# A decoder layer on one core: the first weight tile in two column parts, and the gate multiplications without their order edge from the third block on

## The chip, the core and the metric

One core of one Trainium2 chip. The metric is the time of one execution in device microseconds, the median of several. An execution is one launch of the whole layer, with all weights read from HBM.

## What is computed

One decoder layer for 272 tokens (16 meta tokens and 256 others) of 2048 channels in float32. Cut to what matters here:

```python
h = layer_norm(concat(meta, x))                  # first stage: "h_hl" in the kernel
proj = h @ w_in                                  # 2048 x 8192, 64 weight tiles
a, zh, zb, zc, gates = split(proj)
ya = (pool_mixer(a) @ pool_w * pool_scale) @ pool_proj
yb = (zb * causal_conv(zc * zh)) @ conv_proj
h = layer_norm(alpha * h + (gates[0] * ya + gates[1] * yb) @ w_out)
# PEER: 128 experts per token are picked out of 16384, 16 for each of 8 heads
act = gelu(x . expert_u[idx]);  coef = gate * act
y = sum(coef * expert_v[idx])
out = layer_norm(alpha * h + y)[16:]
```

## The kernel before

**Number format.** Each float32 operand of a large product is split into a high and a low fp32r part (`whi`, `wlo` for weights, `c_hi`, `c_lo` for coefficients, `h_hl`, `x_hl` for activations), and a product is the sum of three: high by high, high by low, low by high. `mm3` (L102 to L104) issues three matmuls for a weight tile and a column range; `mm2` (L108, L109) issues two, the first of them over high and low activations side by side. ACT rounds a raw weight tile to `whi` (L95), DVE or, for some, POOL subtracts to get `wlo` (L74). `load` brings raw tiles of 1 MB into three buffers, issued by SP (L84); `whi` and `wlo` have three buffers of half a tile each.

**The first stage.** DVE normalises the rows. For each of two token tiles (144 tokens with the meta tokens, then 128) and each pair of 128-channel slices `k`, PE transposes into PSUM (L218, L219), ACT applies the norm's scale and shift into `ht` (L222), and DVE writes the high and low part of `h_hl` (L225, L74). Then `in_tile` multiplies the 64 tiles of `w_in`, each over 16 slices `k`. The first of them, with `cols0` = 14, covers columns 14 to 272 of the tokens: 258 columns by `mm3`, 48 matmuls. These want `h_hl` of both token tiles.

**The expert stage.** PEER goes over all 16384 experts as 128 rows of 128. For each row `e` there is an up and a down. The up (`up`) is 32 matmuls of `mm2` over 224 tokens; the 32 tokens left ("lone") are done by gathering rows (`urow`) and working on DVE. `both` (L112, L113) adds the two halves of an up into `gl`, and ACT applies gelu (L625). The down (`product`, L660) is three products of `c_hi`, `c_lo` with a tile of `expert_v`: 12 matmuls of 512 columns per row and half `dh` of the output channels. They accumulate in four banks `acc00` to `acc11`, or `mm` for the second half once the ups are over, and `add` (L669) adds the banks to `res`.

44 ups come ahead. Then the rows go in blocks of four (`NB`): block 0 begins near 957 us. A block is two ups, four downs of the first half, two ups, four downs of the second; ups end near 1830 us, then there are downs alone. `fetch` loads a block's gates `G` as seven DMAs of 64 KB on SP (L745) into one of two buffers. `coef(e)` (from L644) multiplies `gl` by its gate (L648, DVE), then ACT rounds to `c_hi` (L77) and DVE subtracts to `c_lo` (L74); coefficients have five buffers.

**What sets the order.** A scheduler orders each engine's instructions by estimated times and priorities, and each engine then runs its list strictly as it stands. `tc.issue_after(x)` is an edge: what is written in it may not stand ahead of instruction `x` on its engine. In `coef` the edge goes to `last_on["dve"]`, the last weight part or `both` that was recorded for DVE. `fetch(n)` needs a buffer of `Gp` free, so its DMAs wait until the last multiplication of block n - 2 has read it.

Of the kernel before, what the change touches and what calls it, by code (L numbers as in the profile page):

```python
# [18 lines left out]
P = 128  # L19
D = 2048  # L20
KD = D // P
T = 256
NT = T // P
META = 16
TT = T + META
WINDOWS = (2, 4, 8, 16)
# [9 lines left out]
NB = 4  # L36
# [17 lines left out]
def block(ctx, tc, x, meta, w_in, small, pool_w, projs, w_out, wq, keys, eu, eur, ev,  # L54
          ln1_g, ln1_b, ln2_g, ln2_b, lin_g, lin_b, out):
    nc = tc.nc

    def pool(stack, name, bufs, side="left"):
        return stack.enter_context(tc.tile_pool(name=name, bufs=bufs, side=side, reuse_waits="tile"))
# [7 lines left out]
    def ps_mm():  # L67
        return mm.tile([P, 512], F32, name="mm")

    def ps_acc(t, c):  # L70
        return accp.tile([P, 512], F32, name=f"acc{t}{c}")

    def lo_part(lo, full, hi, eng=None):
        return (eng or nc.vector).tensor_tensor(lo, full, hi.bitcast(F32), op=OP.subtract)  # L74

    def split(hi, lo, full):
        nc.scalar.copy(hi, full)  # L77
        lo_part(lo, full, hi)
# [3 lines left out]
    def load(src, shape=None):  # L82
        t = raws.tile([P, 2, 1024], F32, name="raw")
        last_load[0] = nc.sync.dma_start(t if shape is None else shape(t), src).ins  # L84
        return t

    last_lo = [None]
    last_on = {}

    def halves(parts, raw, lo_eng=None, lo_eng1=None, ahead=AHEAD):  # L90
        for s in range(2):
            hi = parts.tile([P, 1024], F32R, name="whi")
            lo = parts.tile([P, 1024], F32R, name="wlo")
            with tc.high_priority(offset=ahead):
                last_on["act"] = nc.scalar.copy(hi, raw[:, s]).ins  # L95
                eng = lo_eng1 if s and lo_eng1 else lo_eng
                last_lo[0] = lo_part(lo, raw[:, s], hi, eng)
                last_on["pool" if eng is nc.gpsimd else "dve"] = last_lo[0].ins
            yield hi, lo

    def mm3(ps, whi, wlo, xhi, xlo, first, last):
        nc.tensor.matmul(ps, whi, xhi, start=first, stop=False)  # L102
        nc.tensor.matmul(ps, whi, xlo, start=False, stop=False)  # L103
        nc.tensor.matmul(ps, wlo, xhi, start=False, stop=last)  # L104

    def mm2(ps, whi, wlo, xhl, first, last):
        n = xhl.shape[-1]
        nc.tensor.matmul(ps[:, :2 * n].rearrange("p (s t) -> p s t", s=2), whi, xhl, start=first, stop=False)  # L108
        nc.tensor.matmul(ps[:, :n], wlo, xhl[:, 0], start=False, stop=last)  # L109
# [60 lines left out]
    with ExitStack() as pa:  # L170
        a1 = pool(pa, "a1", 1, "right")
        parts = pool(pa, "parts", 3)
# [18 lines left out]
                       allow_small_or_imprecise_dtypes=True)  # L191
        nc.gpsimd.memset(neghalf, -0.5)

        h_hl = hp.tile([P, KD, 2, TT], F32R, name="h_hl")
        nc.scalar.activation(neghalf, neghalf, AF.Identity)
        srcs = ((mt[:META], META), (res[:, 0], P), (res[:, 1], P))
# [12 lines left out]
        for t in range(NT):  # L209
            t0, n = (META + P, P) if t else (0, META + P)  # L210
            for k0 in range(0, KD, 2):
                ps = ps_acc(k0 // 2 % 2, k0 // 4 % 2).rearrange("p (k t) -> p k t", k=2)
                ht = a2.tile([P, 2, META + P], F32, name="ht", bufs=4)
                for i in range(2):
                    k = k0 + i
                    ks = slice(k * P, (k + 1) * P)
                    if t == 0:
                        nc.tensor.transpose(ps[:, i, 0:META], mt[:META, ks], ident[:META, :META])  # L218
                    nc.tensor.transpose(ps[:, i, n - P:n], res[:, t, ks], ident)  # L219
                for i in range(2):  # L220
                    k = k0 + i
                    nc.scalar.activation(ht[:, i, :n], ps[:, i, :n], AF.Identity,  # L222
                                         bias=b_in[:, k:k + 1], scale=g_in[:, k:k + 1])
                h_hi = h_hl[:, k0:k0 + 2, 0, t0:t0 + n]
                nc.vector.tensor_copy(h_hi, ht[:, :, :n])  # L225
                lo_part(h_hl[:, k0:k0 + 2, 1, t0:t0 + n], ht[:, :, :n], h_hi)

        lg = lnp.tile([P, D], F32, name="lng")
        lb = lnp.tile([P, D], F32, name="lnb")

        wi = [0]

        later = []

        def in_tile(cols0):
            held = [f for n, f in later if n == 0]
            later[:] = [(n - 1, f) for n, f in later if n]
            ps = ps_mm()
            n = TT - cols0
            raw = load(w_in[wi[0]], lambda t: t.rearrange("p a b -> p (a b)"))  # L240
            wi[0] += 1
            for s, (hi, lo) in enumerate(halves(parts, raw)):
                for kk in range(8):
                    k = s * 8 + kk
                    cs = slice(kk * P, (kk + 1) * P)
                    if n == T:
                        mm2(ps, hi[:, cs], lo[:, cs], h_hl[:, k, :, cols0:], k == 0, k == KD - 1)
                    else:
                        mm3(ps[:, :n], hi[:, cs], lo[:, cs], h_hl[:, k, 0, cols0:], h_hl[:, k, 1, cols0:],
                            k == 0, k == KD - 1)  # L250
            for f in held:
                f()
            return ps if n == T else ps[:, :n]
# [6 lines left out]
        def group_product(g0, w):  # L260
            hi, lo = w
            for g in (g0, g0 + 1):
                for dt in range(2):
                    ps = ps_mm()
                    for ck in range(2):
                        o = (g % 2) * 512 + ck * 256 + dt * P
                        mm3(ps[:, :T], hi[:, o:o + P], lo[:, o:o + P], pooled[g][:, ck, 0], pooled[g][:, ck, 1],
                            ck == 0, ck == 1)
                    n = g * 2 + dt
                    y = a2.tile([P, T], F32, name="y")  # L270
                    nc.vector.tensor_scalar(y, ps[:, :T], scale_c[:, n:n + 1], None, op0=OP.mult)
                    split(ya[:, n, 0], ya[:, n, 1], y)

        for g, w in enumerate(WINDOWS):
            back = max(w, 2)
            a = a2.tile([P, 2, TT], F32, name="a")
            for j in range(2):
                nc.scalar.copy(a[:, j, META - back:], in_tile(META - back))
            prev, width = a, 1
            while width < w:  # L280
                cur = a2.tile([P, 2, TT], F32, name="win", bufs=2)
                lo_t = META - back + 2 * width - 1
                nc.vector.tensor_tensor(cur[:, :, lo_t:], prev[:, :, lo_t:],
                                        prev[:, :, lo_t - width:TT - width], op=OP.add)
                prev, width = cur, 2 * width
            po = a2.tile([P, 2, T], F32, name="po", bufs=1)
            nc.vector.scalar_tensor_tensor(po, prev[:, :, META:], 1.0 / w, a[:, :, META:],
                                           op0=OP.mult, op1=OP.subtract)
            p_hl = a2.tile([P, 2, 2, T], F32R, name="p_hl", bufs=2)
            split(p_hl[:, :, 0], p_hl[:, :, 1], po)  # L290
            pooled[g] = p_hl
            if g == 0:
                praw = load(pool_w, lambda t: t.rearrange("p a b -> p (a b)"))
            if g == 1:
                pw = halves(parts, praw)
            if g % 2 == 1:
                later.append((g // 2, lambda g=g: group_product(g - 1, next(pw))))
# [38 lines left out]
        for m in range(KD):  # L336
# [10 lines left out]
            for (hi, lo), y in zip(halves(parts, praw), (ya, yb)):  # L347
                ps = ps_mm()
                for k in range(NCH):
                    cs = slice(k * P, (k + 1) * P)  # L350
# [13 lines left out]
    with ExitStack() as pw:  # L364
        parts = pool(pw, "parts", 8 + 3)
# [190 lines left out]
    with ExitStack() as pb:  # L556
# [5 lines left out]
        parts = pool(pb, "parts", 3)  # L562
# [81 lines left out]
        def coef(e):  # L644
            gl = gels.pop(e)
            glv = gl.rearrange("p (g t) -> p g t", t=TG)
            with tc.issue_after(last_on["dve"]):
                nc.vector.tensor_tensor(glv, glv, Gs[e // NB][:, :, e % NB], op=OP.mult)  # L648
            c_hi = coefp.tile([P, TD], F32R, name="c_hi")
            c_lo = coefp.tile([P, TD], F32R, name="c_lo")  # L650
            split(c_hi, c_lo, gl)
            coefs[e] = (c_hi, c_lo)
# [248 lines left out]
```

## Time and profile before

| | |
|---|---|
| median of 3 runs | 2117.13 us (2116.28 to 2117.24) |
| profiled execution | 2117.67 us, span 2115.9 us |
| mean granted TensorE clock | 0.988 |
| PE busy | 2054.7 us, 97% |
| DVE busy | 1525.5 us, 72% |
| ACT busy | 1001.8 us, 47% |
| POOL busy | 600.8 us, 28% |
| chain that ended last | PE 90%, DVE 7%, issue, DMA, POOL and ACT 1% each |

The span is the time from the first to the last recorded instruction; the execution's own time has 1.8 us around it. Busy shares are means over stages that differ: the first 24 us and the last 16 us have hardly any matmul, near 700 us top-k work stands between, and in the expert stage PE is almost always busy.

### The profile page before, as it was taken

What the parts mean: (1) busy time and instruction counts of PE and PEld (TensorE: products, weight loads), DVE (VectorE), ACT (ScalarE), POOL (GpSimd) and SP (SyncE); (2) the same over time, 40 slices, a digit from 0 to 9 for tenths busy, and PEclk for the clock granted to TensorE, in tenths of its full rate; (3) what the DMA queues carried; (4) which work ended last, traced back from release to release, by engine and by line L of the source; (5) the groups of instructions that cost most, each with busy time, mean ns of one, the idle gap of its engine ahead of it and who ended that gap; (6) DMA issues with size and microseconds to landing.
All of it is one profiled execution on the core that took longest, in us unless ns stands there. A gap on an engine that the chain in (4) does not pass through costs nothing.

```text
span 2115.9 us, 29922 instructions
## 1 busy us (share of the span) xinstructions
PE 2054.7 (97%) x11558; PEld 1770.5 (84%) x11558; DVE 1525.5 (72%) x2340; ACT 1001.8 (47%) x1424; POOL 600.8 (28%) x294
## 2 busy tenths in 40 slices
PE   7999999999999699999999999999999999999997
PEld 6999888888888689998888888888888888877765
DVE  7766666666779878836767776776677677788878
ACT  5444544444443356554444444444444445444442
POOL 0000000000065588883332333232334232300001
PEclk9999999999999799999999999999999999999998
DMA  5555555566553357787878777878787877877654
GB/s 202 219 180 182 195 181 191 187 224 233 191 183 125 107 202 273 264 284 274 292 266 291 272 269 268 291 269 289 262 283 268 293 260 275 278 271 270 224 169 158
DMA packets 114334, 498.09 MB, mean 235 GB/s; under 512 B 11200, under 2 KB 38336, under 8 KB 73344
## 3 DMA queue, kind: packets, MB, share of 16 engines
q1 hardware_dynamic: 103584, 413.61, 56.8%
q0 software_dynamic: 10608, 82.58, 10.0%
q8 instruction: 90, 1.47, 0.3%
q14 instruction: 52, 0.43, 0.1%
HBM read 478.32 MB, written 16.78 MB: 234 GB/s over the span
## 4 chain that ended last, share of the span: by engine, by line
PE 90%; DVE 7%; issue 1%; DMA 1%; POOL 1%; ACT 1%; SPq 0%; POOLq 0%; ACTq 0%
PE mm L108 28%; PE acc L660 27%; PE mm L109 14%; PE mm L660 5%; PE mm L103 2%; PE mm L102 2%; PE mm L104 2%; PE acc L116 2%; PE acc L117 2%; PE acc L118 2%; PE mm L595 1%; POOL wlo L74 1%; DMA raw<-in_eu 0%; DVE res L669 0%; PE acc L219 0%
## 5 line engine op out<-in xcount | busy, mean ns | idle before, releaser
L95 ACT CAST whi<-raw 128x1024 fp32r<-128x1024 f32 x738 | 772.2, 1048 | 801.5 <-PE mm L108 256.4
L74 DVE TENSOR_TENSOR wlo<-raw,whi 128x1024 fp32r<-128x1024 f32 x546 | 684.7, 1257 | 471.8 <-ACT whi L95 468.3
L108 PE MATMUL mm<-x_hl,whi 128*128 128x448 f32 x2048 | 656.1, 379 | 18.6 <-DVE gl L113 16.8
L74 POOL TENSOR_TENSOR wlo<-raw,whi 128x1024 fp32r<-128x1024 f32 x192 | 490.9, 2563 | 587.1 <-ACT whi L95 282.9
L109 PE MATMUL mm<-x_hl,wlo 128*128 128x224 f32 x2048 | 544.4, 266 | 6.3 <-POOL wlo L74 6.1
L108 PEld LDWEIGHTS mm<-x_hl,whi 128*128 128x128 f32 x2048 | 387.7, 189 | 50.4 <-issue 17.2
L109 PEld LDWEIGHTS mm<-x_hl,wlo 128*128 128x128 f32 x2048 | 394.9, 193 | 10.3 <-POOL wlo L74 8.0
L660 PE MATMUL acc<-whi,c_lo 128*128 128x512 f32 (+1 forms) x832 | 260.7, 395 | 5.0 <-DVE c_lo L74 5.0
L660 PE MATMUL acc<-whi,c_hi 128*128 128x512 f32 (+1 forms) x832 | 260.8, 395 | 4.3 <-ACT c_hi L77 4.3
L660 PE MATMUL acc<-wlo,c_hi 128*128 128x512 f32 (+1 forms) x832 | 260.7, 395 | 0.0
L108 PE MATMUL mm<-h_hl,whi 128*128 128x512 f32 x640 | 225.0, 395 | 0.0
L136 POOL TENSOR_TENSOR rstd<-rstd,neghalf 128x1 f32<-128x1 f32 (+1 forms) x7 | 5.8, 821 | 713.8 <-DVE rstd L135 697.5
L660 PEld LDWEIGHTS acc<-whi,c_lo 128*128 128x128 f32 (+1 forms) x832 | 146.4, 176 | 52.7 <-DVE c_lo L74 6.4
L660 PEld LDWEIGHTS acc<-wlo,c_hi 128*128 128x128 f32 (+1 forms) x832 | 146.2, 176 | 46.1 <-issue 0.2
L660 PEld LDWEIGHTS acc<-whi,c_hi 128*128 128x128 f32 (+1 forms) x832 | 143.0, 176 | 47.5 <-ACT c_hi L77 4.8
L109 PE MATMUL mm<-h_hl,wlo 128*128 128x256 f32 x640 | 180.5, 282 | 0.0
L669 DVE SCALAR_TENSOR_TENSOR res<-res,acc 128x512 f32<-128x512 f32 x208 | 131.6, 679 | 22.6 <-PE acc L660 20.7
L108 PEld LDWEIGHTS mm<-h_hl,whi 128*128 128x128 f32 x640 | 120.4, 188 | 26.9
L625 ACT ACTIVATE gl<-gl 128x224 f32<-128x224 f32 x128 | 49.7, 389 | 168.8 <-DVE gl L113 168.8
L109 PEld LDWEIGHTS mm<-h_hl,wlo 128*128 128x128 f32 x640 | 121.3, 189 | 0.0
L103 PE MATMUL mm<-h_hl,whi 128*128 128x258 f32 (+3 forms) x384 | 110.4, 288 | 0.0
L102 PE MATMUL mm<-h_hl,whi 128*128 128x258 f32 (+3 forms) x384 | 109.3, 285 | 0.0
(189 smaller groups left out, 2586.4 us busy)
## 6 DMA issues: line engine op xcount, KB each, us to landing
raw<-in_eu SPq DMA_DIRECT2D x128, 1024.0 KB, 6.0
raw<-in_ev SPq DMA_DIRECT2D x128, 1024.0 KB, 5.6
raw<-in_w_in SPq DMA_DIRECT2D x64, 1024.0 KB, 4.9
raw<-in_projs SPq DMA_DIRECT2D x16, 1024.0 KB, 4.9
raw<-in_w_out SPq DMA_DIRECT2D x16, 1024.0 KB, 5.0
raw<-in_wq SPq DMA_DIRECT2D x16, 1024.0 KB, 4.8
spill<-wide POOLq DMA_DIRECT2D x7, 2048.0 KB, 7.9
G<-spill SPq DMA_DIRECT2D x212, 64.0 KB, 5.1
```

Source lines behind the costliest of these rows:

```text
L74: return (eng or nc.vector).tensor_tensor(lo, full, hi.bitcast(F32), op=OP.subtract)
L95: last_on["act"] = nc.scalar.copy(hi, raw[:, s]).ins
L102: nc.tensor.matmul(ps, whi, xhi, start=first, stop=False)
L103: nc.tensor.matmul(ps, whi, xlo, start=False, stop=False)
L104: nc.tensor.matmul(ps, wlo, xhi, start=False, stop=last)
L108: nc.tensor.matmul(ps[:, :2 * n].rearrange("p (s t) -> p s t", s=2), whi, xhl, start=first, stop=False)
L109: nc.tensor.matmul(ps[:, :n], wlo, xhl[:, 0], start=False, stop=last)
L116: nc.tensor.matmul(ps, xhi, whi, start=first, stop=False)
L117: nc.tensor.matmul(ps, xhi, wlo, start=False, stop=False)
L625: nc.scalar.activation(gl, gl, AF.Gelu)
L660: nc.tensor.matmul(ps[c][:n_t], c_[:, ts], v_[:, c * 512:(c + 1) * 512], start=e == first and n == 0, stop=e == last and n == 2)
L669: nc.vector.scalar_tensor_tensor(r, r, 1.0 if (t, dh, c) in added else ALPHA, ps[c][:n_t], op0=OP.mult, op1=OP.add)
```

## The change

Two edits. First, a generator `first_tile` multiplies the first tile of `w_in` in two column parts: columns 14 to 144 (130) are written behind the first token tile's transposes, columns 144 to 272 (128) behind the second's. The 48 matmuls of 258 columns become 96. The first `in_tile` call is left out and its bank taken from the generator (`begun`). Second, in `coef` the order edge of the gate multiplication stands only for the first two blocks (`e < 2 * NB`, eight rows); for the other 120 rows the scheduler may place it anywhere behind its inputs.

```diff
+        def first_tile():
+            cols0 = META - max(WINDOWS[0], 2)
+            ps = ps_mm()
+            raw = load(w_in[0], lambda t: t.rearrange("p a b -> p (a b)"))
+            wi[0] = 1
+            parts_ = list(halves(parts, raw))
+            for c0, c1 in ((cols0, META + P), (META + P, TT)):
+                for s, (hi, lo) in enumerate(parts_):
+                    for kk in range(8):
+                        k = s * 8 + kk
+                        cs = slice(kk * P, (kk + 1) * P)
+                        mm3(ps[:, c0 - cols0:c1 - cols0], hi[:, cs], lo[:, cs], h_hl[:, k, 0, c0:c1],
+                            h_hl[:, k, 1, c0:c1], k == 0, k == KD - 1)
+                yield ps[:, :TT - cols0]
...
+            if t == 0:
+                early.append(first_tile())
+            begun = next(early[0])
...
-                nc.scalar.copy(a[:, j, META - back:], in_tile(META - back))
+                nc.scalar.copy(a[:, j, META - back:], in_tile(META - back) if g or j else begun)
...
-            with tc.issue_after(last_on["dve"]):
+            with tc.issue_after(last_on["dve"]) if e < 2 * NB else ExitStack():
                 nc.vector.tensor_tensor(glv, glv, Gs[e // NB][:, :, e % NB], op=OP.mult)
```

PE has 48 matmuls more; all other engines have as many instructions as before. POOL's order is the same. Lines of the changed kernel are 18 or 19 higher (L648 is L667, L745 is L764, L669 is L688), and its tiles carry other numbers.

At the start PE's list now has all 48 matmuls of the first part ahead of the second token tile's transposes but for one pair, and the 48 of the second part among and behind the rest of them. The second tile's matmuls, of which three stood among the first tile's, all come behind.

DVE, at the head of block 0's downs (the first half, second row of the block), before. `wlo_9681` is the second weight tile of this half:

```order
L74 TENSOR_TENSOR wlo_9665<-raw_9662,whi_9664 128x1024
L113 TENSOR_TENSOR gl_9605<-gl_9605,mm_9564 128x224
L74 TENSOR_TENSOR wlo_9681<-raw_9662,whi_9680 128x1024
L74 TENSOR_TENSOR wlo_9699<-raw_9696,whi_9698 128x1024
L113 TENSOR_TENSOR gl_9654<-gl_9654,mm_9611 128x224
L74 TENSOR_TENSOR wlo_9718<-raw_9696,whi_9717 128x1024
L74 TENSOR_TENSOR wlo_9741<-raw_9737,whi_9740 128x1024
L695 ISA urow_9652,act_9716<-urow_9652,lone_9534 128x2048
```
The same place now; `gl_6999` to `gl_7209` are block 2's, `gl_7287` and on block 3's, and `wlo_9729` is the tile that `wlo_9681` was:

```order
L74 TENSOR_TENSOR wlo_9713<-raw_9710,whi_9712 128x1024
L113 TENSOR_TENSOR gl_9653<-gl_9653,mm_9612 128x224
L667 TENSOR_TENSOR gl_6999<-gl_6999,G_9959 128x224
L667 TENSOR_TENSOR gl_7070<-gl_7070,G_9959 128x224
L667 TENSOR_TENSOR gl_7130<-gl_7130,G_9959 128x224
L667 TENSOR_TENSOR gl_7209<-gl_7209,G_9959 128x224
L74 TENSOR_TENSOR wlo_9729<-raw_9710,whi_9728 128x1024
L74 TENSOR_TENSOR wlo_9747<-raw_9744,whi_9746 128x1024
L113 TENSOR_TENSOR gl_9702<-gl_9702,mm_9659 128x224
L667 TENSOR_TENSOR gl_7287<-gl_7287,G_10335 128x224
L74 TENSOR_TENSOR wlo_9766<-raw_9744,whi_9765 128x1024
L667 TENSOR_TENSOR gl_7365<-gl_7365,G_10335 128x224
```
Five gate multiplications now stand ahead of `wlo` tiles of block 0, and more follow; before, none of block 2 stood here.

SP at the same place, before. `G_9911` is block 2's, `raw` tiles are rows of `expert_u` (`in_eu`) or `expert_v` (`in_ev`):

```order
L84 DMA raw_9737<-in_eu 128x2048
L745 DMA G_9911<-spill4_6434 128x128
L745 DMA G_9911<-spill5_6435 128x128
L745 DMA G_9911<-spill6_6436 128x128
L84 DMA raw_9785<-in_eu 128x2048
L84 DMA raw_9836<-in_ev 128x2x1024
L84 DMA raw_9872<-in_ev 128x2x1024
L84 DMA raw_9939<-in_eu 128x2048
```
Now, with `G_9959` as block 2's and `G_10335` as block 3's:

```order
L764 DMA G_9959<-spill4_6482 128x128
L764 DMA G_9959<-spill5_6483 128x128
L764 DMA G_9959<-spill6_6484 128x128
L764 DMA G_10335<-spill0_6478 128x128
L764 DMA G_10335<-spill1_6479 128x128
L764 DMA G_10335<-spill2_6480 128x128
L764 DMA G_10335<-spill3_6481 128x128
L84 DMA raw_9833<-in_eu 128x2048
L764 DMA G_10335<-spill4_6482 128x128
L764 DMA G_10335<-spill5_6483 128x128
L764 DMA G_10335<-spill6_6484 128x128
L84 DMA raw_9884<-in_ev 128x2x1024
```
Block 3's seven loads, which wait for block 2's multiplications on DVE, stand ahead of and between raw tiles that had none ahead of them.

DVE near 2003 us, before, in a block behind the last ups; the `gl` are its coefficients, the `mm` the banks of the block before:

```order
L648 TENSOR_TENSOR gl_16221<-gl_16221,G_18535 128x224
L74 TENSOR_TENSOR wlo_18768<-raw_18749,whi_18767 128x1024
L669 SCALAR_TENSOR_TENSOR res_70<-res_70,mm_18640 128x512
L669 SCALAR_TENSOR_TENSOR res_70<-res_70,mm_18641 128x512
L669 SCALAR_TENSOR_TENSOR res_70<-res_70,mm_18642 96x512
L74 TENSOR_TENSOR wlo_18789<-raw_18786,whi_18788 128x1024
L669 SCALAR_TENSOR_TENSOR res_70<-res_70,mm_18643 96x512
L74 TENSOR_TENSOR c_lo_18727<-gl_16000,c_hi_18726 128x224
L74 TENSOR_TENSOR c_lo_18732<-gl_16048,c_hi_18731 128x224
```
The same block now (its `gl` are `gl_16048`, `gl_16096` and so on):

```order
L74 TENSOR_TENSOR c_lo_18775<-gl_16048,c_hi_18774 128x224
L74 TENSOR_TENSOR wlo_18695<-raw_18692,whi_18694 128x1024
L74 TENSOR_TENSOR wlo_18711<-raw_18692,whi_18710 128x1024
L688 SCALAR_TENSOR_TENSOR res_70<-res_70,acc00_18611 128x512
L688 SCALAR_TENSOR_TENSOR res_70<-res_70,acc01_18612 128x512
L688 SCALAR_TENSOR_TENSOR res_70<-res_70,acc10_18613 96x512
L74 TENSOR_TENSOR wlo_18729<-raw_18726,whi_18728 128x1024
L688 SCALAR_TENSOR_TENSOR res_70<-res_70,acc11_18614 96x512
L728 SCALAR_TENSOR_TENSOR lone_9582<-urow_18543,act_9764,lone_9582 128x2048
L74 TENSOR_TENSOR wlo_18746<-raw_18726,whi_18745 128x1024
L74 TENSOR_TENSOR wlo_18800<-raw_18797,whi_18799 128x1024
L74 TENSOR_TENSOR c_lo_18780<-gl_16096,c_hi_18779 128x224
```
The multiplications are gone from here, and the block's first `c_lo` stands ahead of the adds, with the others spread behind it.

## Rows read from the trace of the kernel before

**Rows 1.** Windows view (length; busy us and count per engine; PEclk, DMA share, GB/s).
```profile
1000.00:1800.00 800.00, 800.00 (x4247) 681.52 (x4246) 564.35 (x691) 380.47 (x532) 275.19 (x126) 1.00 0.78 276
2005.00:2009.10 4.10, 3.63 (x9) 2.76 (x10) 4.00 (x7) 1.54 (x2) 0.00 (x0) 0.58 0.55 183
2032.00:2036.30 4.30, 4.30 (x11) 3.07 (x12) 1.58 (x5) 0.77 (x3) 0.00 (x0) 0.50 0.23 67
```

**Rows 2.** The page, part 5 (busy us, mean ns, idle before and its releaser).
```profile
L660 PE MATMUL acc<-whi,c_lo 128*128 128x512 f32 (+1 forms) x832 | 260.7, 395 | 5.0 <-DVE c_lo L74 5.0
L660 PE MATMUL acc<-whi,c_hi 128*128 128x512 f32 (+1 forms) x832 | 260.8, 395 | 4.3 <-ACT c_hi L77 4.3
```

**Rows 3.** Timeline of PE at the end (start, us, line, out<-in, count, idle before).
```profile
1868.72 1.19 PE L660 MATMUL acc<-whi,c_lo 128*128 128x512 f32 x4 [1.61 <-DVE c_lo L74]
...
2003.02 0.62 PE L660 MATMUL acc<-wlo,c_hi 128*96 128x512 f32 x2
2005.47 1.98 PE L660 MATMUL acc<-whi,c_lo 128*128 128x512 f32 x4 [1.83 <-DVE c_lo L74]
...
2026.92 0.63 PE L660 MATMUL mm<-whi,c_lo 128*96 128x512 f32 x2
2031.85 1.22 PE L660 MATMUL acc<-whi,c_hi 128*128 128x512 f32 x2 [4.30 <-ACT c_hi L77]
```

**Rows 4.** Timeline of DVE at the same places.
```profile
2004.44 0.67 DVE L669 SCALAR_TENSOR_TENSOR res<-res,mm 96x512 f32<-96x512 f32 x1
2005.04 1.28 DVE L74 TENSOR_TENSOR c_lo<-gl,c_hi 128x224 fp32r<-128x224 f32 x4
...
2031.00 0.98 DVE L648 TENSOR_TENSOR gl<-gl,G 128x224 f32<-128x224 f32 x3
```

**Rows 5.** Timeline of SP, the loads of block 2's G.
```profile
961.24 1.76 SPq L745 DMA_DIRECT2D G<-spill  x4
963.86 0.33 SPq L84 DMA_DIRECT2D raw<-in_eu  x1
964.24 1.51 SPq L745 DMA_DIRECT2D G<-spill  x3
```

**Rows 6.** Line L745, landings: the load at 961.24, then that at 965.2.
```profile
DMA to landing us min/median/max: 2.7/2.7/2.7
...
DMA to landing us min/median/max: 9.7/9.7/9.7
```

**Rows 7.** Timeline of DVE behind block 1's coefficients.
```profile
965.16 0.37 DVE L113 TENSOR_TENSOR gl<-gl,mm 128x224 f32<-128x224 f32 x1
966.93 2.36 DVE L74 TENSOR_TENSOR wlo<-raw,whi 128x1024 fp32r<-128x1024 f32 x2 [1.40 <-ACT whi L95]
...
996.03 1.29 DVE L648 TENSOR_TENSOR gl<-gl,G 128x224 f32<-128x224 f32 x4
```

**Rows 8.** Timeline of PE, block 0's downs.
```profile
966.18 0.26 PE L109 MATMUL mm<-x_hl,wlo 128*128 128x224 f32 x1
966.28 0.63 PE L660 MATMUL acc<-whi,c_hi 128*128 128x512 f32 x2
...
969.51 0.62 PE L660 MATMUL acc<-wlo,c_hi 128*128 128x512 f32 x2
...
975.05 0.62 PE L660 MATMUL acc<-wlo,c_hi 128*128 128x512 f32 x2
...
990.62 0.63 PE L660 MATMUL acc<-wlo,c_hi 128*128 128x512 f32 x2
```

**Rows 9.** The page, part 6 (count, size, median us to landing).
```profile
G<-spill SPq DMA_DIRECT2D x212, 64.0 KB, 5.1
```

**Rows 10.** Timeline of PE, first weight tile.
```profile
28.04 0.28 PE L104 MATMUL mm<-h_hl,wlo 128*128 128x258 f32 x1
...
30.90 0.28 PE L104 MATMUL mm<-h_hl,wlo 128*128 128x258 f32 x1
```

**Rows 11.** Timeline of DVE, last of `h_hl`.
```profile
31.15 0.43 DVE L74 TENSOR_TENSOR h_hl<-ht,h_hl 128x256 fp32r<-128x256 f32 x1
```

More of the change, by code (lines that the diff above doesn't have):

```diff
@@ L192, in block @@
         nc.gpsimd.memset(neghalf, -0.5)
+        wi = [0]
+        early = []
+        def first_tile():
[12 more added lines that the diff above has]
+                yield ps[:, :TT - cols0]
         h_hl = hp.tile([P, KD, 2, TT], F32R, name="h_hl")
@@ L226, in block @@
                 lo_part(h_hl[:, k0:k0 + 2, 1, t0:t0 + n], ht[:, :, :n], h_hi)
+            if t == 0:
+                early.append(first_tile())
+            begun = next(early[0])
         lg = lnp.tile([P, D], F32, name="lng")
         lb = lnp.tile([P, D], F32, name="lnb")
-        wi = [0]
         later = []
```

## Prediction

> **What bounds the kernel now.** I read the busy time by stretches first, then the page's instruction groups, then PE, DVE and SP in order of time where PE waits. TensorE is the bound: from 1000 to 1800 us it is busy for all 800.00 us at a full granted clock, with DVE at 564 us [rows 1]. There nothing on another engine is worth anything, unless it comes late enough to stop PE. What is to be had lies outside, in two places.
>
> The first is the end, where the ups are over and only downs are left. The page books 5.0 us of PE idle on `c_lo` and 4.3 us on `c_hi` in the L660 groups [rows 2]. In PE's order of time the 5.0 us are three waits (at 1868.72, 1936.92 and 2005.47; the first and the last are shown), the 4.3 us are one, at 2031.85 [rows 3]. DVE's rows say why. At 2004.44 it adds an `mm` bank to `res`, and only at 2005.04 come the `c_lo` that PE has wanted since about 2003.5. At 2031.00 it begins gate multiplications, whose results ACT has yet to round to `c_hi` [rows 4]. Behind the third and the fourth wait the granted clock lies near half (0.58 and 0.50) for some 4 us each [rows 1].
>
> The second is the first weight tile, for which PE has to wait until `h_hl` is there.
>
> **The gain at the end.** A pair of 512-column matmuls takes 0.46 us, so behind the pair at 2003.02 the next start was due at 2003.48; it came at 2005.47, 1.99 us late (0.16 more than the idle of 1.83 that the row books). Behind 2026.92 it was due at 2027.38 and came at 2031.85, 4.47 us late. The waits at 1868.72 and 1936.92 cost 1.61 + 0.16 = 1.78 us each [rows 3]. That is 10.0 us. A stretch at half clock does half of the work: 4.30 us of busy PE at 0.50 cost 2.15 us, and 3.63 us at 0.58 cost 3.63 x 0.42 = 1.5 us [rows 1]. Together 13.7 us.
>
> After the change the gate multiplications of the last blocks stand hundreds of DVE instructions earlier. A block's first `c_lo` then needs only its `c_hi`, which needs only a free coefficient buffer, and in the changed order it stands ahead of the adds of `mm` (third place shown of the order). I take all 13.7 us; if the adds still come first at one or two of the four places, 7 to 10 us are left of it. So the end is worth -13.7, with -7 as its other bound.
>
> **The loss at the head of the blocks.** Without the order edge the scheduler puts the 36 multiplications of blocks 2 to 10, whose `gl` are ready, and those of 11 and 12 as they come, into the time of blocks 0 and 1. But a G tile has two buffers, and block 1's multiplications come late, so blocks 2 to 6 pass through one buffer, one after the other: last multiplication of a block, seven G issues on SP, landing, first multiplication of the next. DVE takes its instructions in order, and behind each such wait stand `wlo` tiles that PE wants; behind SP's G issues, which now wait for DVE, stand the weight loads.
>
> *Block 2.* Its seven loads stand at the same place of SP's order before and after: four from 961.24, a raw tile at 963.86, three from 964.24, the last of these at 965.2 [rows 5]. The first landed after 2.7 us, the last, behind that raw tile, after 9.7 us [rows 6], at 974.9. Before, nobody waited for it: DVE ended `gl` (L113) at 965.53 and ran the next `wlo` from 966.93 to 968.16 [rows 7], ahead of PE, which came to it at 969.51 [rows 8]. After, four multiplications stand between. They end 1.3 us behind the landing (four took 1.29) at 976.2, the `wlo` (1.23) at 977.4 [rows 7]. PE stands still for 977.4 - 969.51 = **7.9 us**. Nothing covers that, since PE's next matmul needs this very tile.
>
> A rule of the Trainium skill bears on the 9.7 us: "DMA: Bandwidth & Descriptors", section Queues, rings and completion order, has a semaphore's increment land only after all earlier writes of its DMA engine, across its queues. The trace agrees in kind, with 2.7 us ahead of the raw tile and 9.7 behind it. By that rule a wait for G's 64 KB is a wait for the raw tile ahead of it too.
>
> *Block 3.* Its first load is issued at 976.2, the last six issues of 0.44 us and a raw one of 0.33 later [rows 5], at 979.2. I take 5.1 us to landing, the median of all G loads [rows 9]: 984.3. First multiplication 0.4, then `wlo`: 985.9. PE wants that tile at 975.05 + 7.9 = 982.95 [rows 8]: **2.9 us** (0.5 with a landing of 2.7 us, 7.5 with 9.7). *Block 4*, by the same counting, is multiplied just in time for the second half's first `wlo`: 0, up to 3. *Block 5* stands ahead of the `wlo` that PE wants at 990.62 [rows 8] + 10.8 = 1001.4: loads from 996.1 on, landed between 1001.4 and 1003.8, `wlo` 1.5 us later, so 1.5 to 3.9, taken **2.7**. Block 6 stands behind the adds, and its G is there. For *blocks 8 and 9*, in block 1's first down, the counting gives 1.9 to 4.3 and 1 to 2, taken **3.1 and 1.5**. Later blocks have their G a whole block ahead; one multiplication behind each gelu hides, since the next `wlo` waits for ACT anyway.
>
> Sum 7.9 + 2.9 + 2.7 + 3.1 + 1.5 = 18.1, and once the clock, 2.15 as behind the wait of 4.3 us at 2031.85: **20.3 us**. Bounds: with 2.7 us of landing everywhere behind block 2 it is 7.9 + 0.5 + 1.5 + 1.9 + 1 + 2.15 = 15; with 5.1 everywhere, 2 us for block 9 and the clock falling three times, 27. Were block 2's last landing 5.1 us too, its stall would be 3.3 and the sum, with the short ones, some 8.
>
> **The first tile.** 48 matmuls of 258 columns become 96 of 130 and 128. In place, 258 columns run at (30.90 - 28.04)/24 = 0.119 us [rows 10]. The trace has no matmul of this type below 224 columns, which are spaced 0.10 us (966.18 to 966.28) [rows 8]; by its columns a half would take 0.06. So 96 halves cost between 0.1 and 3.9 us more than the 48; I take 0.065 each, 0.5 us, near the lower end, because 224 and 258 columns stand to each other nearly as their columns do. Against it the first part may begin before the second token tile is transposed. But in the changed order all 48 matmuls of the first part, up to its last `k`, stand ahead of most of the second token tile's transposes, so ACT and DVE finish `h_hl` no earlier than now, at 31.58 [rows 11]. Before, PE filled this time with the next weight tile: its 48th matmul started at 30.90 [rows 10], and it went on. After, the first tile ends at about 31.7, some 0.7 us behind, the 0.5 us within it. I take **+0.7**, from -1 (a full clock earlier, transposes not held up) to +3.9.
>
> The Trainium skill speaks against this split: "TensorE: Matmul & The Clock Gate", section Back-to-back issue gap, has about 81 ns for a sustained 128-column matmul with its weight load. By it the 96 would cost 7.8 us in place of my 6.2, and the sum would be 1.6 us higher. No run here shows it.
>
> **The sum** stands against the profiled execution: 2117.67 us, a span of 2115.9 and 1.8 around it. The median of the runs, 2117.13, is 0.5 lower, which I leave aside. 2117.67 - 13.7 + 20.3 + 0.7 = **2125.0 us**. Some 0.2%, 4.2 us, is what a measurement of this kernel tells from no change.
>
> **Rivals.**
> *The waits at the head are short and the end wins: faster.* If G lands in 2.7 us also behind the raw tile, block 2's last load is there at 967.9, its `wlo` is ready at 970.4 and the stall is 0.9; the later ones are 0.5, 1.5, 1.9 and 1, and no clock falls: 5.8 us. 2117.67 - 13.7 + 5.8 + 0.7 = 2110.5. It decides from a head below 8 us. For it speaks that a stalled PE stops the raw loads, and with them the traffic that delays G; against it the 9.7 us at this very place, in an order of SP that stays. 0.20.
> *Gain and loss cancel: no change.* A head of 8 to 17 us, such as 15 with short landings behind block 2: 2117.67 - 13.7 + 15 + 0.7 = 2119.7. 0.27.
> *Slower as forecast:* a head of 17 to 24, 2122 to 2129. 0.38.
> *Much slower:* all landings at 5 us or more and the clock falling behind several stalls, 27 us and over, or the end keeping two of its waits: 2131 and up. 0.15.
> *The change doesn't do what it says:* the last blocks' `c_lo` still stand behind adds at two places, 13.7 - 7 = 6.7 us above the forecast, 2131.7; it is within the last case. The split tile by itself reaches at most +3.9 and decides nothing alone.
>
> **Chances and range.** Faster 0.20, same 0.27, slower 0.53. The forecast's own bounds (head 15 to 27) give 2119.7 to 2131.7. To hold 8 in 10 the range takes in the rival of short waits from 2109 on, and above one more lost wait: 2109 to 2135.
>
> **What would show it.** In the changed kernel's trace: a PE wait of some 8 us near 970 on a `wlo` of DVE, behind a DVE idle that ends with G's landing; smaller ones until about 1035; half clock behind the first. At the end no PE wait on `c_lo` or `c_hi` above 1 us, and a full clock up to 2100. The second weight tile ends within 1 us of its old time. I am wrong if DVE's first wait for G ends before 970, if the early multiplications find their G landed, or if the end keeps its 10 us.

## The result, and the profile after

The changed kernel takes 2142.45 us (median of 4 runs, 2140.57 to 2142.84) against 2116.7 us before: a ratio of 1.0124, 95% interval 1.0109 to 1.0139, some 26 us slower. The forecast was slower by 8 and no more than 18 above.

Where PE stands in its list at five points of the profiled executions (start of the first such matmul; us):

| point | before | after | later by |
|---|---|---|---|
| first product of `p_hl` (the first tiles of `w_in` are done) | 54.57 | 61.95 | 7.38 |
| first down | 966.28 | 973.80 | 7.52 |
| last matmul of the ups | 1831.35 | 1870.16 | 38.81 |
| last down | 2100.23 | 2124.85 | 24.62 |

So the start costs 7.4 us, the head of the blocks 38.8 - 7.5 = 31.3, and the end gives 38.8 - 24.6 = 14.2 back. Between 62 and 974 us the shift stays within 7.3 and 7.7 us, and from 1110 to 1870 us within 0.5 us of 39.

The page now: span, busy times and the groups that answer to [rows 2], with PE's up group for the `wlo` half ahead of them (lines are 19 higher). The second fence has that up group before.

```profile
span 2140.5 us, 30045 instructions
...
PE 2067.0 (97%) x11606; PEld 1778.4 (83%) x11606; DVE 1548.5 (72%) x2340; ACT 1008.4 (47%) x1424; POOL 594.5 (28%) x294
...
L109 PE MATMUL mm<-x_hl,wlo 128*128 128x224 f32 x2048 | 545.0, 266 | 15.0 <-DVE wlo L74 8.0
...
L679 PE MATMUL acc<-wlo,c_hi 128*128 128x512 f32 (+1 forms) x832 | 261.5, 396 | 13.0 <-DVE wlo L74 13.0
L679 PE MATMUL acc<-whi,c_lo 128*128 128x512 f32 (+1 forms) x832 | 260.3, 394 | 0.0
L679 PE MATMUL acc<-whi,c_hi 128*128 128x512 f32 (+1 forms) x832 | 260.3, 394 | 0.0
```
```profile
L109 PE MATMUL mm<-x_hl,wlo 128*128 128x224 f32 x2048 | 544.4, 266 | 6.3 <-POOL wlo L74 6.1
```
The idle on `c_lo` and `c_hi` is gone. New are 13.0 us of waits on DVE's `wlo` in the downs and 8.0 us in the ups (the rest of the 15.0 us there is on POOL's `wlo`, about as before). The windows view of the end (columns as in [rows 1]) shows no gap and a full clock:

```profile
1880.00:1980.00 100.00, 100.00 (x435) 75.79 (x435) 84.08 (x97) 44.51 (x54) 8.66 (x6) 1.00 0.74 256
1980.00:2080.00 100.00, 100.00 (x435) 75.77 (x435) 84.98 (x99) 50.47 (x58) 2.88 (x2) 1.00 0.62 211
```
At the head, DVE's timeline shows the wait that was forecast, and what else was late:

```profile
972.67 0.37 DVE L113 TENSOR_TENSOR gl<-gl,mm 128x224 f32<-128x224 f32 x1
982.52 1.30 DVE L667 TENSOR_TENSOR gl<-gl,G 128x224 f32<-128x224 f32 x4 [9.47 <-issue]
983.73 2.35 DVE L74 TENSOR_TENSOR wlo<-raw,whi 128x1024 fp32r<-128x1024 f32 x2
...
991.43 0.39 DVE L667 TENSOR_TENSOR gl<-gl,G 128x224 f32<-128x224 f32 x1 [5.05 <-DMA G<-spill]
...
1001.73 3.34 DVE L74 TENSOR_TENSOR wlo<-raw,whi 128x1024 fp32r<-128x1024 f32 x1
```
`gl` ends at 973.04 and the four multiplications begin at 982.52, 9.8 us behind the issue of the last G load. That is the 9.7 us of [rows 6] again, but the raw tile ahead of the load is only half of it. In the kernel before, the raw tile issued at 963.86 landed after 4.9 us, and the three G loads behind it [rows 5] after 5.1, 7.4 and 9.7 us. Between the first and the last of them went two gathers of `urow`, 1 MB each, which POOL had issued at 963.98 and 965.31 (256 packets in queue q0 from 968.9 to 974.9 us). The fences show the landings before (views of L84, the raw tile, and of L745, the second and third load), the first gather before, and the DMA queues of the changed kernel from 976 to 981 us (packets, MB, share of the DMA engines; gathers are in q0, G in q1):

```profile
DMA to landing us min/median/max: 4.9/4.9/4.9
...
DMA to landing us min/median/max: 7.4/8.6/9.7
```
```profile
963.98 1.02 POOL L682 DMA_INDIRECT urow<-in_eur,lone_e  x1 [0.15 <-issue]
```
```profile
q0 software_dynamic: 255, 1.95, 92.9%
q1 hardware_dynamic: 270, 0.13, 8.8%
```
For each packet of G, some 0.5 KB, about one of a gather went through, some 7.6 KB. Block 3's last load, behind a raw tile too but with no packet in q0 from 986 to 991.2 us, was issued at 987.06 and multiplied at 991.43, 4.4 us later. No run moved the gathers, so their part is read from the traces, not tested.

PE's timeline, beside [rows 8]:

```profile
976.59 0.62 PE L679 MATMUL acc<-whi,c_hi 128*128 128x512 f32 x2
985.00 1.22 PE L679 MATMUL acc<-wlo,c_hi 128*128 128x512 f32 x2 [7.79 <-DVE wlo L74]
1005.12 0.37 PE L109 MATMUL mm<-x_hl,wlo 128*128 128x224 f32 x1 [2.58 <-DVE wlo L74]
```
The matmul at 985.00 starts 8.2 us behind the second of the pair at 976.59, 8.0 more than the usual 0.23; forecast 7.9. What PE waited for on DVE, in the view of waits (us in total, times, longest):

```profile
PE acc L679 <- DVE wlo L74: 13.0, 6, 7.8
...
PE mm L109 <- DVE wlo L74: 8.0, 4, 2.6
```
And the clock falls four times, not once; the windows view of the four stretches (PEclk is the third column from the right):

```profile
985.00:989.00 4.00, 4.00 (x10) 2.89 (x11) 1.38 (x2) 1.32 (x2) 0.00 (x0) 0.54 0.73 239
1005.00:1009.20 4.20, 4.08 (x16) 3.79 (x17) 2.71 (x7) 0.43 (x2) 3.25 (x1) 0.59 0.74 248
1026.40:1030.00 3.60, 3.57 (x13) 3.34 (x14) 3.60 (x9) 2.51 (x6) 0.80 (x1) 0.55 0.58 180
1046.00:1050.40 4.40, 4.40 (x13) 2.72 (x12) 4.40 (x8) 0.00 (x0) 0.96 (x1) 0.61 0.88 288
```
Summed over PE's starts between 974 and 1110 us, what lies above the usual spacing (0.23 us for 512 columns, 0.31 for an up's pair) is 24.5 us of waits and 7.1 us of matmuls at the lower clock level, 31.6 together. That is the 31.3 us.

At the start, PE's timeline of the first tile:

```profile
24.80 0.41 PE L102 MATMUL mm<-h_hl,whi 128*128 128x130 f32 x1
25.01 0.41 PE L103 MATMUL mm<-h_hl,whi 128*128 128x130 f32 x1
...
30.56 1.93 PE L237 MATMUL acc<-ident,res 128*128 128x128 f32 x8
...
36.01 0.27 PE L103 MATMUL mm<-h_hl,whi 128*128 128x128 f32 x1
36.12 0.28 PE L104 MATMUL mm<-h_hl,wlo 128*128 128x128 f32 x1
```
A matmul of 130 columns takes 0.213 us at 25 us, one of 128 columns 0.111 at 36 us. Before, 258 columns took 0.215 until 25.85 and 0.119 behind it [rows 10]. Half the columns cost nearly the same at either level. The column PEclk reads 1.00 at the start in both kernels, so the level is read off the spacing there; it is the lower until some 33 us now, and was until 25.9 us (the first record of the clock in the two traces, a rise, lies at 33.0 and at 25.9 us).

### The profile page after: what moved, and what is told of

Its sections match the earlier page's. It is cut to its first block, busy times and chain, and to the rows that moved or that the text cites. A ratio compares the mean times of both kernels' runs of the same rounds, so it can differ in the third digit from the quotient of the medians.

```text
span 2140.5 us, 30045 instructions
## 1 busy us (share of the span) xinstructions
PE 2067.0 (97%) x11606; PEld 1778.4 (83%) x11606; DVE 1548.5 (72%) x2340; ACT 1008.4 (47%) x1424; POOL 594.5 (28%) x294
## 4 chain that ended last, share of the span: by engine, by line
PE 87%; DVE 7%; DMA 2%; issue 2%; POOL 1%; SPq 1%; ACT 0%; DVEq 0%; POOLq 0%; ACTq 0%
PE mm L108 27%; PE acc L679 25%; PE mm L109 14%; PE mm L679 6%; PE mm L103 2%; PE mm L102 2%; PE mm L104 2%; PE acc L116 2%; PE acc L118 2%; PE acc L117 2%; PE mm L614 1%; POOL wlo L74 1%; DMA G<-spill 1%; DVE wlo L74 1%; DMA raw<-in_eu 1%
## 5 line engine op out<-in xcount | busy, mean ns | idle before, releaser
L688 DVE SCALAR_TENSOR_TENSOR res<-res,acc 128x512 f32<-128x512 f32 x208 | 131.8, 680 | 26.8 <-PE acc L679 24.4
L103 PE MATMUL mm<-h_hl,whi 128*128 128x258 f32 (+5 forms) x400 | 116.5, 291 | 0.0
L102 PE MATMUL mm<-h_hl,whi 128*128 128x258 f32 (+5 forms) x400 | 115.7, 289 | 0.0
```

Of the source, the lines that this page charges most:

```text
L688: nc.vector.scalar_tensor_tensor(r, r, 1.0 if (t, dh, c) in added else ALPHA, ps[c][:n_t], op0=OP.mult, op1=OP.add)
```

## The experiments

All stand against runs of the kernel before on the same chip (median 2116.1 to 2116.5). The diffs of the parts and of the first tile are against the changed kernel or the kernel with the split alone, those of the look-ahead against the kernel before, as each says. "Start", "head" and "end" are the same three differences of PE's points as in the table above, from the profiled execution.

### One part alone

The split without the other edit (against the changed kernel):

```diff
-            with tc.issue_after(last_on["dve"]) if e < 2 * NB else ExitStack():
+            with tc.issue_after(last_on["dve"]):
```

> The first tile in two column parts, with the order edge kept for all rows. Theory: the delay at the start (the tile begins its third product 7.4 us later in the changed kernel than before, and that shift stays constant up to 950 us) belongs to the split alone: +7.4 us against before, 2124.3. The waits on c_lo and c_hi at the end stay (10 us of late starts). Rival, that the early part only shifts work and the loss comes with the other edit: within 1 us of before.

Measured: 2125.42 us, ratio 1.0045 (1.0029 to 1.0062); start +7.9, head +0.1, end -1.3 (the four waits of [rows 3] are there, but only one of the two falls of the clock). The start's loss belongs to the split. Another -2.5 us came between 680 and 780 us, where a wait of PE for DVE's top-k work near 706 us is 10 to 14 us long from one execution to the next, whatever the kernel.

The edge without the split (against the kernel before):

```diff
-            with tc.issue_after(last_on["dve"]):
+            with tc.issue_after(last_on["dve"]) if e < 2 * NB else ExitStack():
```

> The order edge for two blocks only, the first tile as before. Theory, that the three places add up: head +31.3, end -14.2, so +17 us against before, 2134. PE waits near 978 us of 8 us (7.4 us earlier in time than in the changed kernel). Rival, that half of the head's loss comes from the shifted start (other landings, other collisions): +5 to +10.

Measured: 2134.53 us, ratio 1.0084 (1.0067 to 1.0102); start +0.1, head +32.8, end -14.1. The waits of PE on DVE's `wlo`:

```profile
PE acc L660 <- DVE wlo L74: 16.8, 4, 8.0
...
PE mm L109 <- DVE wlo L74: 6.1, 4, 2.6
```
So the parts add up: alone they give 7.9 + 32.8 - 14.1 = 26.6 us, and both together moved PE's last down by 24.6. The head's loss does not need the late start.

### How far ahead

One block of look-ahead in place of none or all; `marks` holds the last weight part recorded at the start of each block (against the kernel before; `NB` multiplications a block):

```diff
+            marks.append(last_on["dve"])
...
-            with tc.issue_after(last_on["dve"]):
+            with tc.issue_after(marks[e // NB]):
```

> First tile as before; each block's gate multiplications may stand anywhere behind the last DVE weight part recorded at the start of the block before it, so one block of look-ahead, which two G buffers can serve. Theory, that the head's loss is the burst of eleven blocks through two buffers: no burst, no loss, and the end's gain stays: -14 us, 2103. Rival, that any multiplication put ahead of weight parts costs at the head: a loss of 2 to 8 us per block there, the sum near before or above it.

Measured: 2106.89 us, ratio 0.9956 (0.9939 to 0.9973), the profiled execution 11.7 us below that of before; start +0.8, head +0.1, end -14.2, and +1.4 at 965 us, ahead of the first down, where PE waits 2.4 us for a `wlo` of POOL (1.0 before). No multiplication waits for its G. The rival, 2 to 8 us for each block, falls: multiplications ahead of weight parts made PE wait for none of DVE's `wlo` where G is there.

Two blocks of look-ahead. Block 2's multiplications then stand at the place that they have in the changed kernel, and no other block's do (against the kernel before, with the same `marks`):

```diff
-            with tc.issue_after(marks[e // NB]):
+            with tc.issue_after(marks[max(e // NB - 1, 0)]):
```

> First tile as before; two blocks of look-ahead in place of one. In its order block 2's four multiplications stand at the same place as in the changed kernel, behind the first weight part of block 0's down and ahead of the second; block 3's stand a whole block later, and so on, so block 2 is the only one that is multiplied while its G is on the way. Theory, that each wait is the landing of G and that the loss is their sum: one PE wait of 8 us near 977, about 2 us of lower clock behind it, no other wait of DVE on G; with the end's -14 it comes to -4 against before, 2112. Rival, that a wait of 8 us at one place shifts the rest into collisions by itself: +10 or more at the head, and no better than before.

Measured: 2111.22 us, ratio 0.9977 (0.9968 to 0.9987); head +5.1, end -14.2. DVE there:

```profile
962.15 3.36 DVE L74 TENSOR_TENSOR wlo<-raw,whi 128x1024 fp32r<-128x1024 f32 x1
965.43 0.38 DVE L113 TENSOR_TENSOR gl<-gl,mm 128x224 f32<-128x224 f32 x1
972.51 1.30 DVE L648 TENSOR_TENSOR gl<-gl,G 128x224 f32<-128x224 f32 x4 [6.71 <-issue]
973.73 2.35 DVE L74 TENSOR_TENSOR wlo<-raw,whi 128x1024 fp32r<-128x1024 f32 x2
```
The one wait is there, and nothing else on G. It cost 3.3 us and 1.8 of lower clock instead of 8.0 and 2: the last three loads were issued behind the raw tile again, from 964.84 to some 965.8 us, but had landed by 972.51, after 6.7 us in place of the 9.7 of [rows 6]. From 969.7 to 972.3 us q0 moved 113 packets there, fewer than one of the two gathers has (1 MB in rows of 8 KB, 128). PE also waits 2.4 us at 964.5 for a `wlo` of POOL, which took 3.78 us. The mechanism holds; how long the landing takes differs with what the gathers put ahead of it.

The edge for 13 blocks in place of 2, which leaves as many ready blocks to be placed early, but from block 13 on (against the kernel before):

```diff
-            with tc.issue_after(last_on["dve"]):
+            with tc.issue_after(last_on["dve"]) if e < 13 * NB else ExitStack():
```

> First tile as before; the order edge for the first 13 blocks in place of 2. In its order blocks 13 to 23 are multiplied one after the other during block 11. Theory, that the burst of eleven blocks through two buffers is the loss wherever it stands: the head at 970 us is free of waits of DVE, and PE waits on wlo of 8 us and several of 1 to 4 appear near 1420 to 1530; 20 to 32 us in all, the end's -14 stays, so +6 to +18 against before, 2122 to 2134. Rival, that the loss belongs to the head (gathers on POOL, spilled gates just written): no such waits, -14, 2103.

Measured: 2128.69 us in a single run; nothing new at 970 us, end -14.2, and +24.8 us between 1430 and 1520: 18.0 of waits and 7.0 of lower clock by the same sum as above. The first of them on DVE, and on PE:

```profile
1437.02 0.39 DVE L648 TENSOR_TENSOR gl<-gl,G 128x224 f32<-128x224 f32 x1 [5.22 <-DMA G<-spill]
1437.33 1.22 DVE L74 TENSOR_TENSOR wlo<-raw,whi 128x1024 fp32r<-128x1024 f32 x1
```
```profile
1438.60 1.17 PE L660 MATMUL acc<-wlo,c_hi 128*128 128x512 f32 x2 [4.00 <-DVE wlo L74]
```
The burst carries the loss with it, so it is not a property of the head.

Look-ahead of one block only from block 21 on, where there are no ups (against the kernel before, with the same `marks`):

```diff
-            with tc.issue_after(last_on["dve"]):
+            with tc.issue_after(marks[e // NB] if e >= 21 * NB else last_on["dve"]):
```

> First tile as before; the order edge as before for blocks 0 to 20, and one block of look-ahead from block 21 on, where the ups are over. Theory, that the end's four waits are the whole gain: -14 us, 2102, and no change before 1860 us. Against the look-ahead for all blocks it saves the wait of 2.6 us at 965 us. Rival, that some of the gain was from DVE's relief earlier: -9 as with the look-ahead for all, or less.

Measured: 2104.64 us (5 runs), ratio 0.994 (0.9927 to 0.9954): it beats the kernel before and the changed one. The end gives 14.1 us, but the medians differ by 11.6. The intervals of this run and of one block of look-ahead for all rows overlap, so which of the two is faster is not shown. At the end the windows view has neither gap nor lower clock:

```profile
1860.00:1960.00 100.00, 100.00 (x435) 75.80 (x434) 90.32 (x119) 44.71 (x54) 8.66 (x6) 1.00 0.81 276
1960.00:2060.00 100.00, 100.00 (x435) 75.81 (x434) 86.24 (x113) 50.57 (x59) 0.00 (x0) 1.00 0.65 215
```
### The first tile

Four column pieces in place of two (against the split alone, as the next two):

```diff
-            for c0, c1 in ((cols0, META + P), (META + P, TT)):
+            for c0, c1 in ((cols0, 80), (80, META + P), (META + P, 208), (208, TT)):
...
```

> The first tile in four column pieces (66, 64, 64, 64), 192 matmuls; order edge kept. Theory, that a matmul with a weight tile of its own has a floor whatever its columns: 0.111 us apart at the higher clock and 0.213 at the lower one as with 128 and 130 columns, so at the start another 96 matmuls cost 48 x 0.213 + 48 x 0.111 = 15.6 us, some +23 against before. Rival, that below some width each column costs double: 0.056 and 0.107 apart, and the time that of the two-part split, +7.4.

Measured: 2151.57 us in a single run; start +34.0. PE's timeline, early and late in the tile:

```profile
22.82 0.40 PE L102 MATMUL mm<-h_hl,whi 128*128 128x66 f32 x1
23.03 0.40 PE L103 MATMUL mm<-h_hl,whi 128*128 128x66 f32 x1
...
58.09 0.40 PE L102 MATMUL mm<-h_hl,whi 128*128 128x64 f32 x1
58.31 0.40 PE L103 MATMUL mm<-h_hl,whi 128*128 128x64 f32 x1
```
66 and 64 columns cost the 0.213 us of 130 and of 258: a matmul here has a slot that its columns don't shorten. The loss came out 11 us above the expected +23, which had half of the added slots at the higher level, because the clock stayed at the lower level for all 192 of them and rose only at 66.8 us, 2.9 us after the first matmul of 258 columns, though PE had no gap from 44.6 us on; 192 x 0.213 is 40.9 us for one tile.

The two parts with high and low activations side by side, by `mm2` into a bank each and `both` behind it:

```diff
-                        mm3(ps[:, c0 - cols0:c1 - cols0], hi[:, cs], lo[:, cs], h_hl[:, k, 0, c0:c1],
-                            h_hl[:, k, 1, c0:c1], k == 0, k == KD - 1)
+                        mm2(ps, hi[:, cs], lo[:, cs], h_hl[:, k, :, c0:c1], k == 0, k == KD - 1)
...
```

> The first tile in the same two column parts, but each part with the high and low activations side by side: 260 (256) columns and then 130 (128), 64 matmuls in place of 96, and the two halves added afterwards; order edge kept. Theory, that narrow matmuls with a weight tile each both cost a whole slot and leave the clock at its lower level: with every second matmul wide the clock rises earlier than near 33 us (split alone), the first part then runs 0.23 us per k in place of 0.64, and the delay at the start is 0 to +3 us in place of +7.9. Rival, that the clock stays low because real work begins among the transposes: it rises near 33 us again, first part 16 x 0.43 = 6.9 us in place of 10.2, delay +4 to +5.

Measured: 2112.5 us in a single run; start +0.9 (the rest of its 4 us below before came near 706 us, 3.9 us of a shorter wait there, and is no merit of it). PE:

```profile
21.84 0.52 PE L108 MATMUL mm<-h_hl,whi 128*128 128x260 f32 x1
22.16 0.31 PE L109 MATMUL mm<-h_hl,wlo 128*128 128x130 f32 x1
22.27 0.53 PE L108 MATMUL mm<-h_hl,whi 128*128 128x260 f32 x1
...
26.07 0.33 PE L108 MATMUL mm<-h_hl,whi 128*128 128x260 f32 x1
26.23 0.23 PE L109 MATMUL mm<-h_hl,wlo 128*128 128x130 f32 x1
26.30 0.33 PE L108 MATMUL mm<-h_hl,whi 128*128 128x260 f32 x1
```
260 and 130 columns take 0.43 us at first, and 0.23 from 25.3 us on. The clock rises with the wide matmuls, at about the time it did before, and the first part ends at 26.8 us.

Both parts behind the second token tile's transposes:

```diff
-            if t == 0:
-                early.append(first_tile())
-            begun = next(early[0])
...
+        early.append(first_tile())
+        for begun in early[0]:
+            pass
```

> The same two column parts, both written behind the second token tile's transposes; order edge kept. Theory, that the narrow matmuls are the cause wherever they stand: 96 slots of 0.111 to 0.213 us against 48 of 0.12 to 0.215, the delay stays at +4 to +11. Rival, that the place is the cause, the transposes that came too late: delay -1 to +2.

Measured: 2118.51 us in a single run; start +2.9, between the two expectations. The scheduler now put transposes of 128 columns among the first narrow matmuls, and the level rose at 24 us:

```profile
20.39 0.41 PE L103 MATMUL mm<-h_hl,whi 128*128 128x130 f32 x1
20.60 0.41 PE L104 MATMUL mm<-h_hl,wlo 128*128 128x130 f32 x1
...
26.03 0.28 PE L104 MATMUL mm<-h_hl,wlo 128*128 128x130 f32 x1
26.14 0.28 PE L102 MATMUL mm<-h_hl,whi 128*128 128x130 f32 x1
```
So the narrow matmuls cost 2.9 us net when most of them run at the higher level (here they begin at 20.1 us, before the wide ones began at 23.7), and the place of the first part, a stretch from 21.8 to 30.3 us with next to nothing but narrow matmuls, the other 4.5 to 5.

## Why the prediction was wrong, and where it was right

**The end** was right: 13.7 us forecast, 14.2 measured, with all four waits and both falls of the clock gone [rows 3, 4].

**Block 2's wait** was right: 7.9 forecast, 8.0 measured, by the very rows that the sum was made from [rows 6 to 8]. Also right was its mechanism, blocks passing through one buffer with `wlo` tiles queued behind; one block of look-ahead took it away and a shifted edge moved it. Not seen was what makes the landing long: the prediction laid the 9.7 us to the raw tile, which by itself gives 5.1. The number held because the same two gathers stood there again.

**The head as a whole** is the term that was mis-sized: 20.3 forecast with bounds of 15 to 27, 31.3 measured. Behind block 2's wait that is 12.4 forecast and 23.3 measured. Three steps of it failed.

The waits in the downs came out smaller: blocks 3, 5, 7, 8 and 9 cost 0.7, 1.1, 0.9, 2.9 and 0.3 us, 5.9 together, against 2.9, 2.7, 0, 3.1 and 1.5, 10.2. In the main that is because PE came later than the sum had it, held up by the lower clock and by the ups' waits below: it wanted block 3's `wlo` at 992.3 and block 5's at 1014.9, where the sum, moved by the 7.5 us of the start, has 990.5 and 1008.9. The landing was shorter than the assumed 5.1 us for block 3 alone (4.4 us from its last issue to the multiplication; 5.3 for block 5).

The sum counted only `wlo` tiles of the downs and left the ups' out. Besides the blocked multiplications DVE had the gathered rows (`urow`, 2.3 us) and four adds (2.5 us) to catch up with, and the ups' `wlo` came late behind such work: at 997.26, 1005.12, 1026.43 and 1057.76 PE waited 1.6, 2.8, 2.3 and 1.9 us for them, 8.6 in all. The last three of these tiles took DVE 3.34 to 3.41 us in place of 1.23; the first came late because block 3's multiplications ahead of it took 3.20 us, one of them behind POOL in the same way. Each began while POOL was at work; beside the row of 1001.73 above stands this one of POOL:

```profile
1000.89 3.09 POOL L74 TENSOR_TENSOR wlo<-raw,whi 128x1024 fp32r<-128x1024 f32 x1 [5.07 <-ACT whi L95]
```
POOL ends at 1003.98 and DVE at 1005.07, 1.09 us later. The kernel before has 21 such pairs among its 546 `wlo` on DVE, and each ends 1.1 us behind POOL; there DVE was ahead and PE did not feel it. The Trainium skill, "SBUF — State Buffer", section SBUF: two separate sides, has DVE and GpSimd share a pair of ports that the first comer holds for its whole instruction; the trace agrees, with 1.09 us here and 1.1 in the 21 pairs. No run changed this by itself, so what it has in those waits is read, not tested. The remaining 24.5 - 8.0 - 5.9 - 8.6 = 2.0 us are small waits up to 1070 us.

The clock was counted once, 2.15 us. It fell behind four of the waits, those of 8.0, 2.8, 2.3 and 2.9 us, for 7.1 us. The row at 2005.47, a fall behind a wait of 2.0 us, stood in [rows 1, 3] and spoke for more than one; the bound allowed three falls. The length of a wait alone would not have told which ones (last section).

**The first tile** failed in its size, +0.7 forecast with +3.9 as its end, 7.4 measured. The step was "I take 0.065 each, 0.5 us, near the lower end". The rows of 224 columns at 0.10 were taken as a sign that time goes by columns; but each of those matmuls stood behind a wide one. The side-by-side run shows what such a row is worth: there the next matmul follows 130 columns after 0.07 us, yet the wide and the narrow one together take 0.23, two slots of 0.115. Four pieces showed the slot. The bound of 3.9 was near the 2.9 that both parts cost behind the transposes. The rest is that I let the clock rise as before, and the place of the first part: DVE ended `h_hl` at 37.09 us, not at 31.58. The figure of the Trainium skill weighed there ("TensorE: Matmul & The Clock Gate", section Back-to-back issue gap, 81 ns a matmul) was nearer than my 65, and the measurement, 111, lies above both.

**The rival of a faster kernel** fell with the landing: 9.8 us again. The chance for slower was right in sign; of the range, 2109 to 2135, the two mis-sized terms (+11.0 and +6.7) make up the difference of 2142 to the 2125 forecast.

What stays open: what exactly lets the clock rise at the start. With four pieces it stayed low through narrow matmuls, transposes between them now and then up to 44.6 us, until the wide ones came; with both parts behind the second token tile it rose at 24 us, narrow matmuls and transposes in turn. PE was busy in both, and the runs don't separate more than that.

## What to carry to other kernels

An order edge that looks like a mere delay may be what paces the loads behind it: before freeing an instruction, count how many buffers its input has and what is queued behind it on its engine, and free it by fewer blocks than there are buffers (here, with two buffers, one block of look-ahead took the end's gain without the head's loss, and two cost 5.1 us at the head). A wait's price is also what its engine has to catch up with afterwards, and the clock that falls behind it. A matmul that reloads its weight tile should not be split by columns unless the pieces stay wide (here 130 of 258 columns cost as much as all of them).

## What the hardware showed that was not expected

- An fp32r matmul with a weight tile of its own takes 0.111 us at the higher and 0.213 us at the lower level of the clock with 128 or 130 columns, and 0.213 at the lower with 64, 66, 130 and 258; in pairs with a wide one 224 columns were spaced 0.10 [rows 8] and 130 columns 0.11 at the lower and 0.07 at the higher level.
- The clock stayed at its lower level from 17.75 to 66.8 us with four pieces, the last 19 us of narrow matmuls without a gap; with two pieces it rose some 7 us later than before.
- A DVE subtraction that starts inside one of POOL's ends 1.1 us behind it, in all but one case 1.8 to 3.4 us long in place of 1.23 (21 cases before, 12 in the changed kernel).
- Behind a raw tile, G loads of 64 KB landed 2.4 to 2.9 us apart while a gather of 1 MB ran beside them (before, changed, two blocks ahead), and 0.2 us apart with none (block 3 of the changed kernel).
- Behind a wait of PE of 2 to 3 us the clock fell in some places and not in others. In the changed kernel waits of 2.3 to 3 us were followed by 3.6 to 4.4 us at a granted clock near 0.6, and waits of 1.1 to 1.9 us were not. But with the edge alone one of 2.7 us (997.2) was followed by 4 us at 1.00, and so was one of 3.1 us (1508.7) with the edge for 13 blocks. The wait of 2.0 us near 2005 was followed by a fall before and by none with the split alone.
